# The start of a fused decoder layer: first products in two parts by feature chunks, and x scaled on GpSimd

## The chip, the core and the metric

The kernel runs on one core of a Trainium2 chip: TensorE (PE) multiplies, VectorE (DVE), ScalarE (ACT) and GpSimd (POOL) work elementwise, and SyncE (SP) issues nearly all DMA loads. The metric is the device time of one execution in microseconds, lower is better.

## The reference, cut to what matters

One layer: a half-step SwiGLU feed-forward, token mixing, a second feed-forward, each behind an RMS norm that is scaled and shifted by vectors of a conditioning `c`. The change lies at the very start, in the norm and in the first feed-forward's first columns.

```python
m = jax.nn.silu(c) @ w_ada + b_ada
sh1, sc1, g1, sh2, sc2, g2, sh3, sc3, g3 = jnp.split(m[:, None, :], N_MOD, axis=-1)
h = modulate(rms_norm(x, n1_g), sh1, sc1)        # n * (1 + scale) + shift
x = x + 0.5 * g1 * swiglu(h, w1_gate, w1_up, w1_down)
```

There are 512 prompt rows and 8 x 8 sample rows (T = 576 tokens), 1024 features (8 chunks of 128) and 2816 feed-forward columns (22 of 128). Arithmetic is float32.

## The kernel before

**Layout.** Features lie on the partitions and tokens in the free dimension, in two halves of H = 288 tokens. A float32 product is made of three passes of a rounded type: each operand is split into a high part (a copy on ACT, step names ending in h) and a low part (a subtraction on DVE, names in l), and TensorE adds high x high, high x low and low x high: `prod` (line 620) does so for four chunks, 12 matmuls of 128x288.

**Pairs.** A feed-forward step takes one gate and one up column block: a pair. Most pairs save an eighth of the matmuls by seven products of sums of operand blocks (`Pair`, steps P1 to P7). The first two do not (`Plain`, line 676): they make the eight products as they stand, from blocks that need no sums, since the operands are only coming in. The operand blocks, by feature half and token half: N11 is minus the first half's first tokens, N1 the difference of the first half's token halves (tx), B21 and B22 the second half's first and last tokens. For pair i, h0a multiplies N11 (weights n11, n21: steps nh, nl), h1a N1 with the same weights, h0b and h1b multiply B21 and B22 with a12, a22 (steps wh, wl). Each of these is 24 matmuls. T2, N3, N4 are for the later pairs (p2..., P1, ...).

**The norm.** x is loaded row-wise and turned (xt), copied to the feature layout (xc, xS); the row norms are spread over all partitions by a matmul with a matrix of ones (rw, line 1046) and copied out to `rowr` (rr). `xr0` to `xr3` multiply two chunks each by `rowr`, 128x1152, on DVE (`Operands.x`, line 507). Shift and scale come from four parts of w_ada, 2 MB each (`First`): mm0 to mm3 multiply part p by silu(c), M copies the result out, tr turns it, m adds it up on DVE (lines 300, 304, 363). Part p serves chunks 2p and 2p+1: b (ACT) and s (DVE) then scale and shift these. In an operand block, index j stands for two chunks; N11 and N1 have j = 0, 1 (parts 0, 1), B21 and B22 have 2, 3.

**What sets the order.** The string `BEGIN` lists the steps; `run` calls them in that order and binds each of ACT, DVE, PE and GpSimd to it, so each engine works strictly in the order written, and one step that waits holds all behind it on its engine. SyncE issues loads in the order of construction: parts 0 and 1, pair 0's weights (two 512 KB tiles: first and second feature half), part 2, pair 1's weights, part 3, pair 2's. Raw weights lie in three rotating buffers and one of its own, so a load waits until the split that read its buffer is done. After `BEGIN`, from the third pair on, all follows as one stream; there, matmuls that load further conditioning (w_ada strips, line 319) are woven in.

Of the kernel before, what the change touches and what calls it, by code (L numbers as in the profile page):

```python
# [15 lines left out]
P = 128  # L16
# [6 lines left out]
T = NP + NS  # L23
# [13 lines left out]
HALF = (slice(0, H), slice(H, T))  # L37

BEGIN = """
xt0 xt1 xc0 xt2 xc1 xt3 xc2 xt4 xc3 s5 xt5 xc4 r5 r50 r51 r52 xt6 dg xc5 xt7 xc6 rw xS xc7  # L40
rr xr0 xr3 mm0 xr2 M0 tr0 xr1 mm1 m0 nh0 s0 M1 nl0 b00 tr1 b01 m1 wh0 tx0 b10 s1 b11 wl0
N11h0 N11h1 N11l0 N1h0 N11l1 mm2 tx1 N1l0 N1h1 h0a0 T2a1 M2 N1l1 nh1 T2a0 wh1 nl1 tr2 sn0
h1a0 m2 wl1 b20 b21 s2 B21h2 T2b0 B22h2 h0a1 B21l2 T2h0 N3c0 N4c0 N3h0 T2l0 N4h0 N3l0 mm3
B22l2 sn1 N4l0 M3 tr3 h1a1 m3 b30 s3 b31 B21h3 N3c1 p2ah B21l3 T2b1 h0b1 B22h3 p2al p2bh
T2h1 N3h1 N4c1 B22l3 N4h1 p2S h0b0 T2l1 p2U p2bl p2Sh N3l1 h1b0 p2V N4l1 p2Sl e0s0 e0s1 e0m0
e0m1 h1b1 e1a0 p2Uh e1t0 e1s0 p2Ul e1m0 Gh0 P1 e1a1 e1t1 e1s1 Gl0 P2 e1m1 P1s Gh1 Gl1 P5 P6
P5s P6s
"""
INTO_MIX = """
D00 D01 rs00 Wh2 sp00 sq00 ad00 Wl2 D10 rs01 px0 Wh3 sq01 ad01 Wl3 D11 sp01 rs10 sp10 sq10  # L50
# [29 lines left out]
def layer_kernel(ctx: ExitStack, tc: tile.TileContext, a):  # L80
    nc = tc.nc
    PE, DVE, ACT, POOL = nc.tensor, nc.vector, nc.scalar, nc.gpsimd
# [22 lines left out]
    def nm(s):  # L105
        count[0] += 1
        return f"{s}_{count[0]}"
# [5 lines left out]
    def pool(stack, name, side="left"):  # L113
        return stack.enter_context(tc.tile_pool(name=nm(name), bufs=1, side=side, reuse_waits="tile"))
# [14 lines left out]
    def nine(home, shape, dt=F32R):  # L129
        return now[home].tile(shape, dt, tag="x", name=nm(home), bufs=4 if home == "xa" else 3)  # L130
# [4 lines left out]
    def bank():  # L135
        return pp.tile([P, 512], F32, tag="ps", name=nm("ps"), bufs=8)


    def raw4(shape):
        turn[0] += 1  # L140
        own = now["wraw"] is not None and turn[0] % 4 == 0
        return (now["wraw"] if own else wp).tile(
            [P] + shape, F32, tag="wraw", name=nm("wraw"), bufs=1 if own else 3
        )
# [6 lines left out]
    def load_raw(src, k0, kc, c0, cols):  # L151
        raw = raw4([kc, cols])
        nc.sync.dma_start(
            out=raw, in_=src[k0 * P:(k0 + kc) * P, c0:c0 + cols].rearrange("(k p) c -> p k c", p=P)
        )
        return raw
# [52 lines left out]
    def tick(us):  # L209
        for s in list(side):  # L210
            s[1] -= us
            while s in side and s[1] <= 0:
                try:
                    s[1] += next(s[0])
                except StopIteration:
                    side.remove(s)
# [12 lines left out]
    xreg, hreg, greg = ExitStack(), ExitStack(), ExitStack()  # L229
# [4 lines left out]
    def x2(p):  # L234

        return xall[:, 2 * p:2 * p + 2]
# [29 lines left out]
    for i in range(2):  # L266
        for n in range(NT):
            rows = P if n < 4 else NS
            t = first.tile([rows, 512], F32, name=nm("xt"))
# [61 lines left out]
    class First:  # L331

        def __init__(self, p):
            self.p, self.ws = p, []
            for k in range(KC):
                if k % 4 == 0:
                    e = nine("xa" if p < 2 or (p, k) == (3, 4) else "xs1", [P, 4, 512], F32)
                w = e[:, k % 4]
                nc.sync.dma_start(
                    out=w.rearrange("p (m c) -> p m c", m=2),  # L340
                    in_=a["w_ada"][0, k * P:(k + 1) * P, :].rearrange("p (m c) -> p m c", m=9)[
                        :, 0:2, p * 256:(p + 1) * 256],
                )
                self.ws.append(w)
# [126 lines left out]
    def cost(kc):  # L471
        return kc * 3 * 0.1225
# [20 lines left out]
    def op(name):  # L493
        if name not in ops:
            t = nine("xs1" if name in ops["near"] else "xa", [P, 2, 4, H])
            ops[name] = t[:, 0], t[:, 1]
        return ops[name]

    class Operands:
# [6 lines left out]

        def x(self, p, r, cl):
            n = cl.stop - cl.start
            DVE.tensor_tensor(
                out=self.hb[:, 2 * p:2 * p + 2, cl], in0=x2(p)[:, :, cl],  # L510
                in1=r.unsqueeze(1).broadcast_to([P, 2, n]), op=ALU.mult,
            )
# [56 lines left out]
    def operand_steps(O):  # L569
        st = {}  # L570
        for j in range(2):
            for n in ("T2", "N3", "N4", "N1"):
                st[f"{n}h{j}"] = lambda n=n, j=j: O.hi(n, j)
                st[f"{n}l{j}"] = lambda n=n, j=j: O.lo(n, j)
            for n in ("B21", "B22"):
                st[f"{n}h{j + 2}"] = lambda n=n, j=j: O.hi(n, j)
                st[f"{n}l{j + 2}"] = lambda n=n, j=j: O.lo(n, j)
            st[f"N11h{j}"] = lambda j=j: O.hi("N11", j)
            st[f"N11l{j}"] = lambda j=j: O.lo("N11", j)
            st[f"tx{j}"] = lambda j=j: O.tx(j)  # L580
            for n in ("T2a", "T2b", "N3c", "N4c"):
                st[f"{n}{j}"] = lambda n=n, j=j: O.sums(n, j)
        for p in range(4):
            st[f"s{p}"] = lambda p=p: O.s(p)
        return st
# [11 lines left out]
                else:  # L597
                    st[f"b{p}{c}0"] = lambda p=p, c=c: O.b(2 * p + c, HALF[0])

    def pair_steps(p, greg):  # L600

        st = {}

        def G(i, f):
            if now.get("slf") is not greg:
                greg.close()
                now["sl"], now["slots"], now["slf"] = pool(greg, "slf", "right"), FSLOT, greg
            f(i)

        for i in range(2):  # L610
            for n, f in (("nh", "nh"), ("nl", "nl"), ("wh", "wh"), ("wl", "wl"), ("h0a", "h0a"), ("sn", "snaps"),
                         ("h1a", "h1a"), ("h0b", "h0b"), ("h1b", "h1b"), ("e0s", "e0s"), ("e0m", "e0m"),
                         ("e1a", "e1a"), ("e1s", "e1s"), ("e1t", "e1t"), ("e1m", "e1m")):
                st[f"{n}{i}"] = lambda i=i, f=f: getattr(p[i], f)()
            st[f"Gh{i}"] = lambda i=i: G(i, lambda i: p[i].finish_hi())
            st[f"Gl{i}"] = lambda i=i: G(i, lambda i: p[i].finish_lo())
        for n in ("p2ah", "p2al", "p2bh", "p2bl", "p2S", "p2Sh", "p2Sl", "p2U", "p2V", "p2Uh", "p2Ul"):
            st[n] = lambda n=n: getattr(p[2], n[2:])()
        for n, f in (("P1", "p1"), ("P2", "p2"), ("P5", "p5"), ("P6", "p6"), ("P1s", "p1s"), ("P5s", "p5s"), ("P6s", "p6s")):
            st[n] = lambda f=f: getattr(p[2], f)()  # L620
        return st

    def prod(ps, w, x, fresh):
        (wh, wl), (xh, xl) = w, x
        for j in range(4):
            for z, (s, m) in enumerate(((wh, xh), (wh, xl), (wl, xh))):
                PE.matmul(  # L627
                    ps[:, :H], lhsT=s[:, j * P:(j + 1) * P], rhs=m[:, j, :],
                    start=fresh and j == 0 and z == 0, stop=j == 3 and z == 2, skip_group_check=True,
                )  # L630
        tick(cost(4))

    def snap(ps, t=None):
        if t is None:
# [41 lines left out]
    class Plain(Weights):  # L676


        def __init__(self, cols, n):
            self.cols, self.n, self.g, self.w, self.hl, self.raw = cols, n, None, {}, {}, []  # L680
            for z in range(2):
                t = raw4([2, 4, P])
                for i in range(2):
                    self.block_of(t[:, i], i, z)
                self.raw.append(t.rearrange("p m k c -> p m (k c)"))

        def nh(self):
            self.put_hi(("n11", "n21"), self.raw[0], True)
# [226 lines left out]
    class Down:  # L915
# [5 lines left out]
        def load(self, c):  # L921
            if c not in self.raw:
                self.raw[c] = load_raw(self.wd, self.f0, self.n, c * P, P)
# [72 lines left out]

    w1 = a["w1_gate"][0], a["w1_up"][0]
    a1 = lines(cst, [P, KC, 9], name="a1")
    parts = [First(0), First(1)]
    def cols(w, f):  # L1000
        return (w[0], f * P), (w[1], f * P)

    pairs = {0: Plain(cols(w1, 0), 0)}
    parts.append(First(2))
    pairs[1] = Plain(cols(w1, 1), 1)
    parts.append(First(3))
    pairs[2] = Pair(cols(w1, 2))
    junk = ada_tile()
    for i in range(2):
        for n in range(NT):  # L1010
            m = P if n < 4 else NS
# [18 lines left out]
    s5, r5, t5 = (lines(tp, [P, NT], tag=f"n{i}", name=f"n{i}", bufs=1) for i in range(3))  # L1030
    rowr = tp.tile([P, T], F32, tag="all", name="rowr", bufs=1)
    dg, psR = [], []
# [31 lines left out]
            return getattr(O1(), name)  # L1064

    ops["near"] = ("B21", "B22", "N3")
    steps = {**operand_steps(Late()), **pair_steps(pairs, greg)}
    for c in range(KC):
        steps[f"xt{c}"] = lambda c=c: turn_x(c)
        steps[f"xc{c}"] = lambda c=c: DVE.tensor_copy(out=xs[c][:, 0:NP], in_=psX[c])  # L1070
# [31 lines left out]
    tok_pools, st, xxreg = ExitStack(), ExitStack(), ExitStack()  # L1102
# [609 lines left out]
    for i in range(2):  # L1712
        for n in range(NT):
            m, z = P if n < 4 else NS, NT * i + n
# [71 lines left out]
    xt2 = []  # L1786
# [17 lines left out]
    for pr in ([0], [1], [2], [3], [4], [5], [6, 7]):  # L1804
# [4 lines left out]
        for h in range(2):  # L1809
            for c in pr:  # L1810
                ps = proj(W[c], OA, h)
                t = sa[c][:, HALF[h]]
# [22 lines left out]
    ffn2, st = ExitStack(), ExitStack()  # L1835
    hreg, greg = ExitStack(), ExitStack()
# [19 lines left out]
    pairs = {0: Plain(cols(w2, 0), 0), 1: Plain(cols(w2, 1), 1), 2: Pair(cols(w2, 2))}  # L1856
    steps = {**operand_steps(O), **pair_steps(pairs, greg)}
# [173 lines left out]
```

## Time and profile before

| | us |
|---|---|
| median of 3 runs (1686.89 to 1688.15) | 1687.76 |
| the profiled execution | 1688.23 |
| its span, first to last instruction | 1686.4 |
| TensorE busy | 1650.3 (98%) |
| VectorE busy | 1157.2 (69%) |
| ScalarE busy | 785.5 (47%) |
| GpSimd busy | 290.6 (17%) |
| chain that ended last: TensorE's share | 91% |

The chain that ended last is followed back from the last instruction, each step to what released it. It is almost all TensorE, with DMA 3%. A busy TensorE is not TensorE at its peak, since matmuls are pipelined; start-to-start times tell more than the length of one.

### The profile page before, as it was taken

What the parts mean: (1) busy time and instruction counts of PE and PEld (TensorE: products, weight loads), DVE (VectorE), ACT (ScalarE), POOL (GpSimd) and SP (SyncE); (2) the same over time, 40 slices, a digit from 0 to 9 for tenths busy, and PEclk for the clock granted to TensorE, in tenths of its full rate; (3) what the DMA queues carried; (4) which work ended last, traced back from release to release, by engine and by line L of the source; (5) the groups of instructions that cost most, each with busy time, mean ns of one, the idle gap of its engine ahead of it and who ended that gap; (6) DMA issues with size and microseconds to landing.
All of it is one profiled execution on the core that took longest, in us unless ns stands there. A gap on an engine that the chain in (4) does not pass through costs nothing.

```text
span 1686.4 us, 31365 instructions
## 1 busy us (share of the span) xinstructions
PE 1650.3 (98%) x12548; PEld 1589.0 (94%) x12548; DVE 1157.2 (69%) x1835; ACT 785.5 (47%) x1331; POOL 290.6 (17%) x372
## 2 busy tenths in 40 slices
PE   8999999999999999999999999999999999999997
PEld 4899999999999998899999999998999999999997
DVE  6767847576697776754687654676848868676773
ACT  6533524344564565553444444443236525343453
POOL 0000000000411110113335442444231000000002
PEclk9999999999999999999999999999999999999999
DMA  9443444332547675665457475789540333232331
GB/s 317 130 149 101 139 142 121 113 114 85 166 127 226 202 217 170 210 197 180 127 180 241 156 171 170 205 232 283 182 138 3 96 91 95 87 96 77 100 88 57
DMA packets 300213, 252.09 MB, mean 149 GB/s; under 512 B 13594, under 2 KB 260634, under 8 KB 300067
## 3 DMA queue, kind: packets, MB, share of 16 engines
q1 hardware_dynamic: 284594, 206.76, 40.2%
q0 software_dynamic: 13168, 40.97, 8.8%
q10 hardware_dynamic: 2304, 2.36, 0.4%
q8 instruction: 98, 1.61, 0.4%
q14 instruction: 49, 0.39, 0.1%
HBM read 207.01 MB, written 43.02 MB: 148 GB/s over the span
## 4 chain that ended last, share of the span: by engine, by line
PE 91%; DMA 3%; DVE 2%; issue 1%; ACT 1%; SPq 1%; POOL 0%; DVEq 0%; POOLq 0%; ACTq 0%
PE ps L627 46%; PE ps L461 29%; PE ps L1325 5%; PE ps L1553 2%; PE ps L283 2%; PE ps L1453 1%; PE ps L1336 1%; PE ps L1415 1%; DMA xa<-in_w_ada_dram 1%; PE ps L1459 1%; PE ps L1431 0%; PE ps L1353 0%; PE ps L295 0%; DMA c<-in_gm_ln_g_dram 0%; DMA c<-accd 0%
## 5 line engine op out<-in xcount | busy, mean ns | idle before, releaser
L627 PE MATMUL ps<-xa,whl 128*128 128x288 f32 x3000 | 429.5, 298 | 4.5 <-ACT whl L645 1.4
L627 PEld LDWEIGHTS ps<-xa,whl 128*128 128x128 f32 x3000 | 410.1, 190 | 17.3 <-issue 5.9
L627 PE MATMUL ps<-xs,whl 128*128 128x288 f32 x2040 | 294.1, 297 | 4.0 <-ACT sn L636 4.0
L627 PEld LDWEIGHTS ps<-xs,whl 128*128 128x128 f32 x2040 | 278.8, 189 | 13.9 <-ACT sn L636 6.8
L655 DVE TENSOR_TENSOR whl<-wraw,whl 128x1024 fp32r<-128x1024 f32 x192 | 234.6, 1225 | 57.5 <-ACT whl L645 50.3
L645 ACT CAST whl<-wraw 128x1024 fp32r<-128x1024 f32 x192 | 200.4, 1048 | 104.0 <-DVE wraw L769 60.2
L461 PE MATMUL ps<-c,wd 128*128 128x288 f32 x1824 | 246.1, 295 | 0.0
L461 PEld LDWEIGHTS ps<-c,wd 128*128 128x128 f32 x1824 | 242.9, 188 | 3.4 <-issue 3.4
L461 PE MATMUL ps<-c,whl 128*128 128x288 f32 x1368 | 191.6, 297 | 4.3 <-DVE S L1492 3.2
L461 PEld LDWEIGHTS ps<-c,whl 128*128 128x128 f32 x1368 | 183.3, 188 | 7.0 <-DVE S L1492 3.9
L448 POOL TENSOR_TENSOR x<-x,s 128x64 f32<-128x64 f32 x72 | 35.0, 487 | 817.0 <-DVE s L447 789.5
L442 DVE SCALAR_TENSOR_TENSOR x<-ps,gate,x 128x288 f32<-128x288 f32 (+1 forms) x128 | 61.2, 481 | 119.3 <-PE ps L461 119.3
L165 DVE TENSOR_TENSOR whl<-wraw,whl 128x1024 fp32r<-128x1024 f32 x56 | 80.1, 1433 | 72.5 <-ACT whl L164 70.0
L636 ACT COPY sn<-ps 128x288 f32<-128x288 f32 x195 | 77.6, 398 | 109.4 <-PE ps L627 108.5
L928 ACT CAST wd<-wraw 128x640 fp32r<-128x640 f32 (+2 forms) x58 | 45.3, 781 | 106.7 <-PE ps L461 102.1
L1325 PE MATMUL ps<-whl,xx 128*128 128x256 f32 x768 | 91.6, 279 | 0.0
L1325 PEld LDWEIGHTS ps<-whl,xx 128*128 128x128 f32 x768 | 90.7, 188 | 0.0
L164 ACT CAST whl<-wraw 128x1024 fp32r<-128x1024 f32 x56 | 58.6, 1048 | 28.2 <-PE ps L461 16.0
L627 PE MATMUL ps<-xs,whs 128*128 128x288 f32 x480 | 70.1, 294 | 0.0
L645 ACT CAST whs<-wraw 128x512 fp32r<-128x512 f32 x62 | 38.4, 620 | 66.1 <-PE ps L627 58.9
L627 PEld LDWEIGHTS ps<-xs,whs 128*128 128x128 f32 x480 | 65.7, 188 | 0.0
L933 DVE TENSOR_TENSOR wd<-wraw,wd 128x640 fp32r<-128x640 f32 (+2 forms) x58 | 53.4, 921 | 9.0 <-ACT wd L928 8.6
(285 smaller groups left out, 2226.6 us busy)
## 6 DMA issues: line engine op xcount, KB each, us to landing
ada<-in_w_ada_dram SPq DMA_DIRECT2D x56, 512.0 KB
wraw<-in_w_in_dram SPq DMA_DIRECT2D x96, 256.0 KB
wraw<-in_w_gate_dram SPq DMA_DIRECT2D x88, 256.0 KB
wraw<-in_w_up_dram SPq DMA_DIRECT2D x88, 256.0 KB
wraw<-in_w_in_dram SPq DMA_DIRECT2D x32, 512.0 KB
wraw<-in_w_down_dram SPq DMA_DIRECT2D x32, 384.0 KB
wraw<-in_w_down_dram SPq DMA_DIRECT2D x32, 320.0 KB
accd<-c POOLq DMA_DIRECT2D x32, 288.0 KB, 5.5
```

Source lines behind the costliest of these rows:

```text
L164: ACT.copy(out=hi, in_=raw)
L165: (eng or DVE).tensor_tensor(out=lo, in0=raw, in1=hi.bitcast(F32), op=ALU.subtract)
L442: DVE.scalar_tensor_tensor(out=x[:, o:o + w], in0=ps[:, :w], scalar=g[:, c, 0:1], in1=x[:, o:o + w], op0=ALU.mult, op1=ALU.add)
L448: return lambda: POOL.tensor_tensor(out=x[:, NP:T], in0=x[:, NP:T], in1=u, op=ALU.add)
L461: PE.matmul(ps[:, :H], lhsT=s[:, k, c0:c0 + P], rhs=m[:, HALF[h]], start=k == 0 and z == 0, stop=k == kc - 1 and z == 2,)
L627: PE.matmul(ps[:, :H], lhsT=s[:, j * P:(j + 1) * P], rhs=m[:, j, :], start=fresh and j == 0 and z == 0, stop=j == 3 and z == 2, skip_group ...
L636: ACT.copy(out=t, in_=ps[:, :H])
L645: ACT.copy(out=hl[:, 0], in_=src)
L655: DVE.tensor_tensor(out=hl[:, 1], in0=src, in1=hl[:, 0].bitcast(F32), op=ALU.subtract)
L928: ACT.copy(out=hl[:, 0], in_=self.raw[c])
L933: DVE.tensor_tensor(out=lo, in0=self.raw[c], in1=hi.bitcast(F32), op=ALU.subtract)
L1325: PE.matmul(ps[:, :DV], lhsT=s, rhs=m, start=i == 0, stop=i == 23)
```

## The change

Four things, all before 80 us. (1) Each product of the first two pairs is cut in two by feature chunks: h0a has only the chunks j = 0, h0c those of j = 1, h1a and h1c likewise; h0b, h0d, h1b, h1d for the second half. Each is 12 matmuls; their number and sum stay the same. (2) The pairs' weights are loaded part by part: first halves behind parts 0 and 1, second halves behind parts 2 and 3. (3) `BEGIN` is written anew. (4) `xr1`, `xr2`, `xr3` run on GpSimd, `xr0` stays on DVE; the later norms, which call `x` by token halves, stay on DVE too.

```diff
-            DVE.tensor_tensor(
+            (POOL if p and cl.stop == T and not cl.start else DVE).tensor_tensor(
                 out=self.hb[:, 2 * p:2 * p + 2, cl], in0=x2(p)[:, :, cl],
...
-    def pair_steps(p, greg):
+    def pair_steps(p, greg, parted=False):
...
         for i in range(2):
+            if parted:
+                for n in ("h0a", "h0c", "h0b", "h0d", "h1a", "h1c", "h1b", "h1d"):
+                    st[f"{n}{i}"] = lambda i=i, n=n: p[i].part(n)
...
-                st[f"{n}{i}"] = lambda i=i, f=f: getattr(p[i], f)()
+                st.setdefault(f"{n}{i}", lambda i=i, f=f: getattr(p[i], f)())
...
-    def prod(ps, w, x, fresh):
+    def prod(ps, w, x, fresh, js=range(4)):
...
-        for j in range(4):
+        for j in js:
...
-        tick(cost(4))
+        tick(cost(len(js)))
...
+        def part(self, name):
+
+            t = "AD"[int(name[1])]
+            z, js = {"a": (0, (0, 1)), "c": (0, (2, 3)), "b": (1, (0, 1)), "d": (1, (2, 3))}[name[2]]
+            if name[2] == "a":
+                setattr(self, t, [bank() for _ in range(2)])
+            x = (("N11", "B21"), ("N1", "B22"))[int(name[1])][z]
+            for ps, w in zip(getattr(self, t), (("n11", "n21"), ("a12", "a22"))[z]):
+                prod(ps, self.w[w], op(x), z == 0, js)
...
-    parts = [First(0), First(1)]
...
-    pairs = {0: Plain(cols(w1, 0), 0)}
-    parts.append(First(2))
-    pairs[1] = Plain(cols(w1, 1), 1)
-    parts.append(First(3))
+    pairs, parts = {i: Plain(cols(w1, i), i, ()) for i in range(2)}, []
+    for p in range(4):
+        parts.append(First(p))
+        pairs[p % 2].load(p // 2)
     pairs[2] = Pair(cols(w1, 2))
```

In the lists below, each row is an instruction with its line, output<-inputs and size; line numbers of the changed kernel differ a little. TensorE before, from the ones matmul to the first products (xa_150 and xa_155 are part 0, the next two part 1, xs_28 and xs_29 part 2; xa_370 with whl_343 is h0a of pair 0):

```order
L1046 MATMUL ps_295<-h_284,ones 128x64
L283 MATMUL ps_312<-xa_150,cs 32x512 x4
L283 MATMUL ps_312<-xa_155,cs 32x512 x4
L295 MATMUL ps_324<-ident,ada_322 128x128 x4
L283 MATMUL ps_330<-xa_160,cs 32x512 x4
L283 MATMUL ps_330<-xa_165,cs 32x512 x4
L295 MATMUL ps_351<-ident,ada_347 128x128 x4
L283 MATMUL ps_377<-xs_28_176,cs 32x512 x4
L283 MATMUL ps_377<-xs_29_181,cs 32x512 x4
L627 MATMUL ps_390<-xa_370,whl_343 128x288 x12
```

And now (xa_350 is N11, xa_376 is N1, whl_321 the weights n11 and n21):

```order
L282 MATMUL ps_294<-xa_155,cs 32x512 x4
L1061 MATMUL ps_303<-h_276,ones 128x128
L1061 MATMUL ps_303<-h_278,ones 128x128
L1061 MATMUL ps_303<-h_280,ones 128x128
L1061 MATMUL ps_303<-h_282,ones 128x128
L1061 MATMUL ps_304<-h_284,ones 128x64
L294 MATMUL ps_314<-ident,ada_310 128x128 x4
L282 MATMUL ps_336<-xa_163,cs 32x512 x4
L282 MATMUL ps_336<-xa_168,cs 32x512 x4
L294 MATMUL ps_354<-ident,ada_352 128x128 x4
L630 MATMUL ps_362<-xa_350,whl_321 128x288 x6
L630 MATMUL ps_363<-xa_350,whl_321 128x288 x6
```

mm0 has moved ahead of the ones matmuls, and the first products ahead of mm2. VectorE before, at the multiplications by the norms (hb is the normed x, m, mT and a belong to step m0, whl to nl0):

```order
L509 TENSOR_TENSOR hb_309<-x_90,rowr 128x1152 x4
L300 TENSOR_REDUCE m_339<-ps_324 128x36
L304 TENSOR_TENSOR mT<-m_339,vec 128x2x18
L363 SCALAR_TENSOR_TENSOR a_149<-mT,vec 128x18
L525 TENSOR_TENSOR hb_309<-hb_309,a_149 128x2x64
L525 TENSOR_TENSOR hb_309<-hb_309,mT 128x2x64
L651 SCALAR_TENSOR_TENSOR whl_343<-wraw_170,whl_343 128x1024
```

And now; the other three multiplications stand on GpSimd as `L508 TENSOR_TENSOR hb_331<-x_90,rowr 128x1152 x3`, with nothing ahead of them but the memsets of the start:

```order
L299 TENSOR_REDUCE m_323<-ps_314 128x36
L303 TENSOR_TENSOR mT<-m_323,vec 128x2x18
L362 SCALAR_TENSOR_TENSOR a_149<-mT,vec 128x18
L508 TENSOR_TENSOR hb_331<-x_90,rowr 128x1152
L654 SCALAR_TENSOR_TENSOR whl_321<-wraw_160,whl_321 128x1024
L524 TENSOR_TENSOR hb_331<-hb_331,a_149 128x2x64
L524 TENSOR_TENSOR hb_331<-hb_331,mT 128x2x64
L546 SCALAR_TENSOR_TENSOR xa_350<-hb_331,xa_350 128x576
```

m0 has moved ahead of x0, and one multiplication is left on VectorE. ScalarE before, where wh1 stands (`whl_423`, right behind nh1 `whl_420`; ada_417 is M2, sn are copies of finished products):

```order
L289 COPY ada_417<-ps_377 128x512
L643 ACTIVATE whl_420<-wraw_186 128x1024
L645 CAST whl_423<-wraw_189 128x1024
L636 COPY sn_431<-ps_390 128x288
L636 COPY sn_433<-ps_391 128x288
```

And now (ada_540 is M3, the two activations are b30 and b31, whl_576 is wh1, xs_82 is B21h3):

```order
L288 COPY ada_540<-ps_531 128x512
L541 CAST xs_89_544<-hb_331 128x576
L541 CAST xa_556<-hb_331 128x576
L515 ACTIVATE hb_331<-hb_331,mT,a_149 128x512 x2
L648 CAST whl_576<-wraw_199 128x1024
L541 CAST xs_82_493<-hb_331 128x576
```

wh1 has moved behind M3 and behind b30 and b31.

More of the change, by code (lines that the diff above doesn't have):

```diff
@@ L39 @@
 BEGIN = """
[L40 to L47, printed above, removed]
+xt0 xt1 xc0 xt2 xc1 xt3 xc2 xt4 xc3 s5 xt5 xc4 r5 r50 r51 r52 xt6 dg xc5 xt7 xc6 mm0 rw M0 xS xc7 tr0
+rr nh0 m0 xr0 xr1 xr2 xr3 mm1 nl0 b00 b01 s0 N11h0 M1 tr1 N11l0 tx0 h0a0 N1h0 m1 N1l0 b10 b11 s1 h1a0
+N11h1 N11l1 tx1 N1h1 h0c0 N1l1 nh1 sn0 nl1 h1c0 mm2 M2 T2a0 T2a1 h0a1 wh0 tr2 m2 h0c1 wl0 b20 b21 s2
+B21h2 B21l2 sn1 B22h2 T2b0 h0b0 B22l2 T2h0 N3c0 h1b0 mm3 M3 N4c0 T2l0 N3h0 tr3 N3l0 m3 N4h0 b30 b31
+h1a1 s3 wh1 N4l0 B21h3 wl1 B21l3 h1c1 B22h3 N3c1 B22l3 h0b1 p2ah T2b1 h0d0 p2al T2h1 h1d0 p2bh N3h1 T2l1
+h1b1 N4c1 h0d1 e0s0 p2S N3l1 N4h1 e0s1 p2U e0m0 p2bl p2Sh h1d1 N4l1 e0m1 p2V e1a0 p2Sl p2Uh
+e1t0 e1s0 p2Ul P1 e1m0 Gh0 e1a1 e1t1 e1s1 Gl0 P2 e1m1 P1s Gh1 Gl1 P5 P6 P5s P6s
 """
@@ L676, in layer_kernel, with __init__, load @@
     class Plain(Weights):
-        def __init__(self, cols, n):
+        def __init__(self, cols, n, halves=range(2)):
             self.cols, self.n, self.g, self.w, self.hl, self.raw = cols, n, None, {}, {}, []
[L681 to L685, printed above, removed]
+            for z in halves:
+                self.load(z)
+        def load(self, z):
+            t = raw4([2, 4, P])
+            for i in range(2):
+                self.block_of(t[:, i], i, z)
+            self.raw.append(t.rearrange("p m k c -> p m (k c)"))
+        def part(self, name):
[6 more added lines that the diff above has]
+                prod(ps, self.w[w], op(x), z == 0, js)
         def nh(self):
@@ L1066, in layer_kernel @@
     ops["near"] = ("B21", "B22", "N3")
-    steps = {**operand_steps(Late()), **pair_steps(pairs, greg)}
+    steps = {**operand_steps(Late()), **pair_steps(pairs, greg, True)}
     for c in range(KC):
```

## The prediction, made before the changed kernel had run

> **What bounds the kernel now.** I read the busy times by stretch first: they cut the start at the places where TensorE's work changes. Columns: stretch, its length, busy time of each engine, then the granted clock, the DMA share and GB/s.
>
> ```profile
> core 0: us, PE busy (x) PEld busy (x) DVE busy (x) ACT busy (x) POOL busy (x), PEclk, DMA share, GB/s
> 18.40:34.50 16.10, 14.19 (x67) 5.06 (x66) 15.57 (x27) 8.96 (x14) 0.00 (x0) 1.00 1.06 345
> 34.50:46.60 12.10, 12.10 (x93) 10.46 (x92) 9.09 (x16) 7.56 (x12) 0.00 (x0) 1.00 1.08 345
> 46.60:49.20 2.60, 0.65 (x9) 0.59 (x6) 2.10 (x3) 1.77 (x5) 0.00 (x0) 1.00 0.92 302
> 49.20:52.60 3.40, 3.40 (x16) 3.40 (x15) 2.23 (x7) 2.48 (x4) 0.00 (x0) 0.50 0.59 155
> 52.60:66.60 14.00, 14.00 (x106) 14.00 (x106) 13.33 (x21) 8.03 (x12) 0.00 (x0) 1.00 0.14 40
> 66.60:115.80 49.20, 49.20 (x363) 44.33 (x362) 33.32 (x52) 24.14 (x41) 0.00 (x0) 1.00 0.47 137
> ```
>
> From 18.4 to 49.2 the DMA engines are full (share 0.92 to 1.08); VectorE is full until 34.5 (15.57 of 16.10); GpSimd does nothing. From 52.6 on TensorE has no gap. So the change can move the time only by when TensorE gets through the first two pairs: what it is late there, it is late at the end. The next view is TensorE in order of time (start, duration, what, and in brackets the idle time before).
>
> ```profile
> 18.08 0.37 PE L1024 MATMUL ps<-ident,xt 64*128 64x64 f32 x1
> 18.37 2.69 PE L1046 MATMUL ps<-h,ones 128*128 128x128 f32 x10
> 20.99 2.33 PE L283 MATMUL ps<-xa,cs 128*32 128x512 f32 x16
> 24.12 0.66 PE L295 MATMUL ps<-ident,ada 128*128 128x128 f32 x4 [0.79 <-ACT ada L289]
> 24.70 1.92 PE L283 MATMUL ps<-xa,cs 128*32 128x512 f32 x16
> ...
> 32.88 1.71 PE L283 MATMUL ps<-xs,cs 128*32 128x512 f32 x4 [0.27 <-DMA xs<-in_w_ada_dram]
> 34.52 3.46 PE L627 MATMUL ps<-xa,whl 128*128 128x288 f32 x24
> 37.81 0.60 PE L295 MATMUL ps<-ident,ada 128*128 128x128 f32 x4
> 38.17 6.63 PE L627 MATMUL ps<-xa,whl 128*128 128x288 f32 x48
> ...
> 48.61 0.66 PE L295 MATMUL ps<-ident,ada 128*128 128x128 f32 x4 [1.96 <-ACT ada L289]
> 49.02 4.96 PE L627 MATMUL ps<-xa,whl 128*128 128x288 f32 x24
> 53.82 12.96 PE L627 MATMUL ps<-xs,whl 128*128 128x288 f32 x96
> 66.62 1.76 PE L627 MATMUL ps<-xa,whl 128*128 128x288 f32 x12
> ```
>
> The first product stands at 34.52, behind the third part's DMA; the two pairs have 24+48+24+96 = 192 product matmuls; the third pair begins at **66.62**. 96 of them take 66.62 - 53.82 = 12.80 (0.133 each), 48 take 6.56 (0.137): I use 0.1345. Check: 34.52 + 192 x 0.1345 (25.8) + mm3 1.9 + two turns 1.1 + the wait 1.96 + what the half clock adds to 24 matmuls (4.80 to the next start, against 3.3: 1.5) = 66.8, against 66.62. This sum, made again for the new order, is the forecast.
>
> **The change: the first product without GpSimd's price.** Prices of the small steps:
>
> ```profile
> 20.48 0.59 ACT L1051 COPY rowr<-ps 128x512 f32<-128x512 f32 x1 [3.48 <-PE ps L1046]
> 21.10 0.21 ACT L1052 COPY rowr<-ps 128x64 f32<-128x64 f32 x1
> 39.23 1.52 ACT L516 ACTIVATE hb<-hb,mT,a 128x512 f32<-128x512 f32 x2 [0.82 <-DVE a L363]
> 33.98 0.67 ACT L542 CAST xa<-tx 128x576 fp32r<-128x576 f32 x1 [1.08 <-DVE tx L559]
> 34.62 0.59 ACT L289 COPY ada<-ps 128x512 f32<-128x512 f32 x1
> 28.73 1.03 ACT L645 CAST whl<-wraw 128x1024 fp32r<-128x1024 f32 x1
> 21.34 5.16 DVE L509 TENSOR_TENSOR hb<-x,rowr 128x1152 f32<-128x1152 f32 x4 [0.28 <-ACT rowr L1052]
> 38.45 0.31 DVE L300 TENSOR_REDUCE m<-ps 128x36 f32<-128x144 f32 x1 [0.69 <-PE ps L295]
> 38.79 0.20 DVE L304 TENSOR_TENSOR mT<-m,vec 128x36 f32<-128x36 f32 x1
> 39.02 0.18 DVE L363 SCALAR_TENSOR_TENSOR a<-mT,vec 128x18 f32<-128x18 f32 x1
> 39.53 1.23 DVE L655 TENSOR_TENSOR whl<-wraw,whl 128x1024 fp32r<-128x1024 f32 x1 [0.33 <-issue]
> 40.67 0.28 DVE L525 TENSOR_TENSOR hb<-hb,a 128x128 f32<-128x128 f32 x1
> 42.07 0.75 DVE L551 TENSOR_TENSOR xs<-hb,xs 128x576 fp32r<-128x576 f32 x1
> ```
>
> mm0 now stands ahead of rw on TensorE. Together they took 18.37 to 23.3 and still do, but rowr is copied out at 23.4 to 24.2, 2.9 us later than at 20.48. tr0 ends at 24.0, m0 (0.31 + 0.20 + 0.18 with links, 0.75) at 24.9, x0 (5.16 / 4 = 1.29) at 26.2, b00 and b01 (1.52) at 27.7, N11h0 (0.67) at 28.4. Behind it on ScalarE M1 (0.59) ends at 29.0 and tr1 on TensorE at 29.7; N11l0 (0.75) is done at 29.2. First product: **29.7**, 4.8 earlier than now, because it needs neither the second half of the chunks nor m2.
>
> **GpSimd's three multiplications.** They replace 3 x 1.29 on VectorE. The trace has no 128x1152 row on GpSimd; the nearest are additions of 128x576, with VectorE beside them:
>
> ```profile
> 769.54 0.75 DVE L1302 TENSOR_TENSOR c<-c,rope 128x576 f32<-128x576 f32 x1
> 770.20 3.56 DVE L165 TENSOR_TENSOR whl<-wraw,whl 128x1024 fp32r<-128x1024 f32 x2
> 773.93 0.69 DVE L1355 TENSOR_TENSOR c<-ps,hc 128x512 f32<-128x512 f32 x1 [0.17 <-PE ps L1353]
> ```
>
> ```profile
> 770.36 2.31 POOL L1303 TENSOR_TENSOR c<-c,c 128x576 f32<-128x576 f32 x1 [1.88 <-DVE c L1302]
> 772.74 1.17 POOL L1383 COPY h<-c 128x128 f32<-128x128 f32 x1
> ```
>
> Two instructions of 1.23 take 3.56 beside GpSimd: 1.1 to 1.2 us more than two alone. GpSimd starts at 770.36, within the first, takes 2.31 and ends at 772.67; the first of the two is over by 771.4. I read it as turn-taking: VectorE's first, then GpSimd's whole addition (about 1.3), then VectorE's second, which had to stand still. The 0.69 row, with an operand in PSUM, is as long as ever. The Trainium skill's "GPSIMD Engine Reference", section "Specifications", says that GpSimd shares its SBUF interfaces with VectorE, with contention for VectorE instructions that have two SBUF inputs; it gives no price for the wait. These rows agree. Without that rule the sum below ends at +0.7 us, with it at +8.2.
>
> A 128x1152 multiplication is then, as an estimate from these rows, 2 x 1.3 to 1.35, 2.7 us (bounds: 0 for VectorE if nothing is shared, 2 x 2.31 = 4.6 if the whole row counts; I take 2.7, since the rest of the 2.31 is GpSimd's own wait). All three are ready when rowr is there, at 24.2. VectorE then has mT, a, x0, nl0, s0 (two) and N11l0 to do before the first product, all with two SBUF operands, and they alternate: GpSimd's x1 to 26.9, mT, x2 to 29.8, a, x3 to 32.6, x0 to 33.9. Queued behind mT is all of VectorE, and ScalarE and TensorE wait for that. Then b00, b01 to 35.4, N11h0 36.1, M1 36.6, tr1 and with it the first product at **37.2**: 2.7 later than now, not 4.8 earlier.
>
> **From the first product to the third pair.** h0a0 runs to 38.8. h1a0 waits for tx0, N1h0, N1l0 (0.75 + 0.67 + 0.75, to 39.0): 0.3 idle. h0c0 waits for b10, b11, N11h1, N11l1, to 41.3: 0.6. h1c0 waits for tx1, N1h1, N1l1: 0.6. Now mm2, h0a1, tr2, h0c1 run to 50.8, but h0b0 needs B21l2, and from the end of tr2 (49.2) that is m2 0.75, b20 and b21 1.52, B21h2 0.67, B21l2 0.75 and links 0.4: 53.3, **2.5 idle**; only h0c1 (1.6) covers it. h0b0, h1b0, mm3 run to 58.4; tr3 waits 0.8 for M3. h1a1 and h1c1 run to 63.0; h0b1 needs wl1, and on ScalarE wh1 (1.03) stands behind b30 and b31, on VectorE wl1 (1.23) behind it: m3, b30, b31, wh1, wl1 end at 65.1, **2.1 idle**. The six parts left, with no wait, are 9.7.
>
> Sum: 37.2 + 25.8 + mm2 and mm3 3.8 + two turns 1.1 + waits (0.3 + 0.6 + 0.6 + 2.5 + 0.8 + 2.1 = 6.9) = **74.8** against 66.6: +8.2 us. The third pair then follows with no new wait: laid out by the same rows, its p2al, p2bl and p2Sl are ready 6, 3 and 1.5 us ahead.
>
> **Moves that I cost at nothing.** SyncE's loads: 512 KB of weights now stand ahead of part 1, at 345 GB/s 1.5 us; mm1 ends near 26, and tr1 is not due before 29.7. Part 2 lands as before (33.5 by the 32.88 row), mm2 comes at 45. Part 3 lands 1.5 us earlier, to no use: mm3 comes at 56. The early landing is not what TensorE waits for any more; without the cover of the late start, part 1's delay would cost 1.5. Pair 3's second weight tile is queued behind the two w_ada strips, whose buffers wait for tr2 and tr3 (59.8), and for wl1 (65.1); it lands near 68 and is wanted near 77.
>
> **Rivals.** (1) *GpSimd costs VectorE nothing*: first product 29.7, the same 37.6 behind it, 67.4, **+0.7**. For it: nothing but that a multiplication by a broadcast row may pass otherwise than these additions. Against: the 3.56. (2) *Faster*: the early start is kept, if there is no turn-taking and the waits in front of h0b0 and h0b1 (4.6) and the small ones shrink to 1.5, as VectorE has 3.9 us less to do: 62, **-4.6**. It decides at a chain from tr2 to B21l2 below h0c1's 1.6; the rows make it 4.1, in the trace of before too. (3) *Part of the turns*: one or two of three fall behind VectorE's work: **+3 to +6**. (4) *Half clock*: now 1.96 idle is followed by 3.4 us at 0.50, at a cost of 1.5; the idle times of 2.5 and 2.1 may each bring one: **up to +11**. The Trainium skill's "TensorE: Matmul & The Clock Gate", Part 1, lets the clock fall after an idle window of about 3.4 us: by it these two cost nothing, and only the 10 us ahead of the first product would, hidden in the small waits. The row of 1.96 speaks against so strict a reading.
>
> **The numbers.** The profiled execution took 1688.23 (span 1686.40), 0.5 above the median of 1687.76. Forecast +8.2: 1696.4 by that execution, 1696.0 as a median. Chances: forecast 0.48, (4) 0.16, (3) 0.12, (1) 0.14, (2) 0.10. The range goes from (1), 1688.0, to (4), 1699.5; below it lies (2), above it some of (4). A measurement tells 0.2%, 3.4 us, from no change: slower 0.74, same 0.16, faster 0.10.
>
> **What would show it.** Right: VectorE's mT, a and x0 rows stretched to 2 us and more beside three GpSimd rows between 24 and 33 us; first product near 37; waits of over 2 us ahead of h0b0 and h0b1; third pair near 75. Wrong: mT at 0.2 us and a first product at 30; or a TensorE without those two waits.

## The result, and the profile after

The changed kernel takes 1694.74 us (median of 4 runs, 1694.71 to 1695.94) against 1687.35 for the kernel before (4 runs beside it): a ratio of 1.0048, 95% interval 1.0036 to 1.006, or 7.4 us more. Run again later beside other experiments it had the same ratio, 1.0048 (1.0035 to 1.006). The profiled execution took 1695.94, with a span of 1694.2 where the kernel before had 1686.4.

TensorE of the changed kernel in order of time (start, duration, what, idle time before and what ended it):

```profile
18.99 3.64 PE L282 MATMUL ps<-xa,cs 128*32 128x512 f32 x16
22.56 1.56 PE L1061 MATMUL ps<-h,ones 128*128 128x128 f32 x10
...
24.63 1.92 PE L282 MATMUL ps<-xa,cs 128*32 128x512 f32 x16
33.89 1.11 PE L294 MATMUL ps<-ident,ada 128*128 128x128 f32 x4 [7.33 <-ACT ada L288]
34.65 0.59 PE L630 MATMUL ps<-xa,whl 128*128 128x288 f32 x1
35.92 8.34 PE L630 MATMUL ps<-xa,whl 128*128 128x288 f32 x47 [0.68 <-DVE xa L546]
44.19 1.92 PE L282 MATMUL ps<-xs,cs 128*32 128x512 f32 x16
...
51.51 0.40 PE L630 MATMUL ps<-xs,whl 128*128 128x288 f32 x1 [1.56 <-ACT xs L541]
52.30 4.83 PE L630 MATMUL ps<-xs,whl 128*128 128x288 f32 x23 [0.40 <-DVE xs L550]
...
59.78 0.66 PE L294 MATMUL ps<-ident,ada 128*128 128x128 f32 x4 [0.79 <-ACT ada L288]
...
64.35 0.53 PE L630 MATMUL ps<-xs,whl 128*128 128x288 f32 x2 [0.33 <-ACT whl L648]
65.61 9.59 PE L630 MATMUL ps<-xs,whl 128*128 128x288 f32 x70 [0.73 <-DVE whl L658]
75.04 1.76 PE L630 MATMUL ps<-xa,whl 128*128 128x288 f32 x12
```

The first product comes at 34.65, almost where it came before (34.52), and the third pair at 75.04 instead of 66.62. That is 8.4 us later, and the span grew by 7.8: the loss lies in the first 75 us. The stretches between these rows (length, busy time of each engine, granted clock, DMA share, GB/s):

```profile
core 0: us, PE busy (x) PEld busy (x) DVE busy (x) ACT busy (x) POOL busy (x), PEclk, DMA share, GB/s
18.40:34.65 16.25, 8.92 (x53) 3.77 (x52) 11.97 (x10) 4.92 (x8) 9.01 (x3) 0.84 1.10 375
34.65:44.19 9.54, 8.86 (x51) 8.27 (x49) 7.38 (x16) 5.10 (x8) 0.00 (x0) 0.73 0.75 244
44.19:52.30 8.11, 6.15 (x46) 4.27 (x45) 4.20 (x10) 4.57 (x8) 0.00 (x0) 1.00 0.30 88
52.30:57.07 4.77, 4.77 (x24) 4.61 (x24) 3.29 (x5) 1.00 (x2) 0.00 (x0) 0.64 0.62 187
57.07:75.04 17.97, 15.99 (x118) 13.79 (x117) 13.29 (x23) 11.78 (x17) 0.00 (x0) 1.00 0.21 59
75.04:124.24 49.20, 49.20 (x359) 43.98 (x358) 37.20 (x59) 24.91 (x43) 0.00 (x0) 1.00 0.49 148
```

In the 49.20 us behind 75.04 TensorE has no gap, as before behind 66.62. From the first product to the third pair there lie 192 matmuls of 0.1345 us (25.8), mm2 and mm3 (3.8) and two turns (1.1), 30.7 in all; the stretch took 40.39, so 9.7 is waits and half clock. Before, mm2 stood ahead of the first product, and the same stretch was 32.10 for 28.8 of work: 3.3. The loss is thus 0.1 (first product) + 1.9 (mm2, now inside) + 6.4. VectorE and GpSimd ahead of the first product:

```profile
24.74 0.31 DVE L299 TENSOR_REDUCE m<-ps 128x36 f32<-128x144 f32 x1 [4.21 <-PE ps L294]
25.08 2.19 DVE L303 TENSOR_TENSOR mT<-m,vec 128x36 f32<-128x36 f32 x1
27.31 2.52 DVE L362 SCALAR_TENSOR_TENSOR a<-mT,vec 128x18 f32<-128x18 f32 x1
29.75 1.34 DVE L508 TENSOR_TENSOR hb<-x,rowr 128x1152 f32<-128x1152 f32 x1
31.01 3.65 DVE L654 SCALAR_TENSOR_TENSOR whl<-wraw,whl 128x1024 fp32r<-128x1024 f32 x1
...
35.11 0.75 DVE L546 SCALAR_TENSOR_TENSOR xa<-hb,xa 128x576 fp32r<-128x576 f32 x1
```

```profile
24.57 9.01 POOL L508 TENSOR_TENSOR hb<-x,rowr 128x1152 f32<-128x1152 f32 x3 [22.59 <-DMA xa<-in_w_ada_dram]
```

mT, a and nl0 took 0.20, 0.18 and 1.22 before; now 2.19, 2.52 and 3.65, 6.8 more, while GpSimd works on its three multiplications (9.01 in all). x0 between them keeps its 1.34.

### The profile page after: what moved, and what is told of

Read it like the earlier page. It is cut to its first block, busy times and chain, and to the rows that moved or that the text cites. A ratio compares the mean times of both kernels' runs of the same rounds, so it can differ in the third digit from the quotient of the medians.

```text
span 1694.2 us, 31383 instructions
## 1 busy us (share of the span) xinstructions
PE 1649.6 (97%) x12548; PEld 1588.8 (94%) x12548; DVE 1159.3 (68%) x1832; ACT 784.2 (46%) x1331; POOL 299.7 (18%) x375
## 4 chain that ended last, share of the span: by engine, by line
PE 85%; issue 6%; DMA 4%; DVE 3%; ACT 1%; POOL 1%; SPq 1%; POOLq 0%; DVEq 0%; ACTq 0%
PE ps L630 39%; PE ps L460 30%; PE ps L1340 5%; PE ps L1568 2%; PE ps L282 1%; PE ps L1468 1%; PE ps L1351 1%; PE ps L1430 1%; DMA c<-x1d 1%; DMA xa<-in_w_ada_dram 1%; PE ps L1474 1%; DMA accd<-c 1%; PE ps L1446 0%; PE ps L1368 0%; DMA c<-in_gm_ln_g_dram 0%
```

## The experiments

Theory T: GpSimd's turns, and where the multiplications, mm2 and wh1 stand, make the loss. Rival O: GpSimd costs VectorE nothing; the order alone loses. Rival C: half clock, which the changed kernel has for 10.24 us from 29.49 and for 3.41 from 53.38 (before: 3.41 from 49.18). Rival P: cutting the products is what loses. All ratios are to the kernel before, on the same chip. The third pair's start, and the time at half clock ahead of it, are those of one profiled execution of each kernel.

| run | third pair at, us | half clock ahead of it, us | ratio | 95% interval |
|---|---|---|---|---|
| before | 66.62 | 3.41 | 1 | |
| changed | 75.04 | 13.65 | 1.0048 | 1.0036 to 1.006 |
| e8, changed again | 72.78 | 10.24 | 1.0048 | 1.0035 to 1.006 |
| e1, x on VectorE | 70.34 | 6.83 | 1.0034 | 1.0022 to 1.0046 |
| e2, before with GpSimd | 66.06 | 0 | 1.0012 | 1.0004 to 1.0021 |
| e3, rows first | 72.88 | 10.24 | 1.005 | 1.0038 to 1.0062 |
| e4, TensorE kept busy | 74.13 | 3.41 | 1.0065 | 1.0051 to 1.0079 |
| e5, x ahead of its use | 68.12 | 3.41 | 1.0012 | 1.0003 to 1.0022 |
| e6, and wh1 early | 65.79 | 3.41 | 0.9996 | 0.9987 to 1.0005 |
| e7, order by rows | 60.91 | 0 | 0.9969 | 0.9956 to 0.9981 |
| e9, e7 with GpSimd | 65.64 | 6.83 | 1.0007 | 0.9997 to 1.0018 |

In the extracts of `BEGIN` below, lines are shortened to the steps that move.

**e1: the multiplications back on VectorE.**

```diff
-            (POOL if p and cl.stop == T and not cl.start else DVE).tensor_tensor(
+            DVE.tensor_tensor(
```

> The changed kernel with the three multiplications x1 to x3 back on VectorE, at the same places. Theory T (GpSimd's turns stretch VectorE's instructions): mT and a back at 0.2 us, VectorE has 3 x 1.29 = 3.9 us more of its own but loses 2.0 + 2.3 + 2.4 = 6.7 us of stretching; the first product near 32.5 instead of 34.65, the third pair near 70.5 to 71.5 instead of 75.0, so 3.5 to 4.5 us faster than the changed kernel, still 3 to 4 us slower than the kernel before. Rival O (GpSimd costs VectorE nothing, the order alone makes the loss): VectorE is 3.9 us longer ahead of the first product, up to 3.9 us slower than the changed kernel. Rival C (half clock): no change beyond what the half-clock stretches do; the loss stays while there are 13.6 us of half clock.

VectorE of this run:

```profile
23.94 0.20 DVE L303 TENSOR_TENSOR mT<-m,vec 128x36 f32<-128x36 f32 x1
24.17 0.18 DVE L362 SCALAR_TENSOR_TENSOR a<-mT,vec 128x18 f32<-128x18 f32 x1
24.57 5.16 DVE L508 TENSOR_TENSOR hb<-x,rowr 128x1152 f32<-128x1152 f32 x4 [0.23 <-DMA wraw<-in_w_gate_dram]
29.66 1.22 DVE L654 SCALAR_TENSOR_TENSOR whl<-wraw,whl 128x1024 fp32r<-128x1024 f32 x1
```

The stretching is gone and nl0 ends at 30.88, not 34.66, though VectorE does three multiplications more. One matmul of the first product runs at 29.14, the others from 32.13, 3.8 earlier than in the changed kernel. The third pair is 4.7 earlier than in the first profile of the changed kernel and 2.4 earlier than in the second; like this run, the second has no half clock behind the wait ahead of h0b0. O, which had this run slower, falls. But the ratio is still 1.0034: without GpSimd the new order loses too.

**e2: only GpSimd, in the old order.** The same edit as the change's, in the kernel before.

> The kernel before with nothing but x1 to x3 on GpSimd. Theory T: mT, a and an instruction behind them are stretched by some 2 us each, the third pair starts near 69.5 instead of 66.6, 2 to 4 us slower than before. Rival O: VectorE is relieved of 3.9 us, no change or up to 2 us faster.

```profile
26.09 1.41 DVE L304 TENSOR_TENSOR mT<-m,vec 128x36 f32<-128x36 f32 x1
27.53 2.54 DVE L363 SCALAR_TENSOR_TENSOR a<-mT,vec 128x18 f32<-128x18 f32 x1
```

In these rows of VectorE the two instructions are stretched by 1.2 and 2.4, less than the 3.9 that VectorE is spared, and the first product comes at 34.76, where it came before at 34.52. The expected 69.5 was too late: in the old order part 2's load and mm2 stand ahead of the first product and cover most of it. What is left is 0.9 us, by which the turn behind the first 24 products starts later (38.74 against 37.81). The ratio says 0.4 to 2.1 in a thousand slower, but the third pair is 0.6 earlier, because this profile has no half clock behind the 1.96 us of idle time, worth 1.5 before. T's sign holds by the times; its size was over-estimated.

**e3: rows ahead of mm0.**

```diff
-xc6 mm0 rw M0 xS xc7 tr0
-rr nh0 m0
+xc6 rw mm0 xS xc7 rr M0
+tr0 nh0 m0
```

> The changed kernel with the ones matmuls (rw) and the copies of rowr ahead of mm0 and M0, as before the change. rowr is there 2.9 us earlier, so GpSimd's first multiplication falls into VectorE's idle time in front of m0 and takes no turn from it. Theory T: one turn less, the third pair near 72.3, 2 to 3 us faster than the changed kernel. Rival O: the multiplications were not what the first product waited for, less than 1 us. Rival C: no change.

```profile
25.18 0.31 DVE L299 TENSOR_REDUCE m<-ps 128x36 f32<-128x144 f32 x1 [4.61 <-PE ps L294]
25.52 1.08 DVE L303 TENSOR_TENSOR mT<-m,vec 128x36 f32<-128x36 f32 x1
26.64 2.51 DVE L362 SCALAR_TENSOR_TENSOR a<-mT,vec 128x18 f32<-128x18 f32 x1
29.08 1.34 DVE L508 TENSOR_TENSOR hb<-x,rowr 128x1152 f32<-128x1152 f32 x1
30.35 1.21 DVE L654 SCALAR_TENSOR_TENSOR whl<-wraw,whl 128x1024 fp32r<-128x1024 f32 x1
```

The turns went as T said: GpSimd's first multiplication (from 21.31) falls into VectorE's idle time, mT loses only 0.9, and nl0 nothing. The time is a miss all the same: ratio 1.005, no better. mm0 now waits behind rw, and m0 starts at 25.18, against 24.74 and 23.14 in the two profiles of the changed kernel. Against the first of them the third pair is 2.2 earlier, about as expected. Against the second it is no earlier: VectorE's last split ahead of mm2 ends at 40.41, only 0.5 before its 40.87, and a half-clock stretch ahead of the third pair, worth 1.5, fell into this profile and not into that one. Against this second profile, then, the later m0 takes back most of what the earlier rowr wins, and the times show no gain.

**e4: TensorE kept busy.**

```diff
-rr nh0 m0 xr0 xr1 xr2 xr3 mm1 nl0
+rr nh0 m0 xr0 xr1 xr2 xr3 mm1 dm0 nl0
...
-tr2 m2 h0c1 wl0
+tr2 m2 h0c1 dm1 wl0
...
+        for _ in range(20):
+            PE.matmul(parts[1].p2[:, 0:P], lhsT=ones, rhs=ident, start=True, stop=True)
...
+        for _ in range(4):
+            PE.matmul(pairs[1].A[0][:, H:H + P], lhsT=ones, rhs=ident, start=True, stop=True, skip_group_check=True)
```

The second batch is written with `start=True` into the bank in which pair 1's first sums are being added up. The output suggests that this starts the bank's sum anew, so that a part of pair 1's product is left out.

> The changed kernel with matmuls of ones by the identity, whose results nobody reads, in two of TensorE's idle times: 20 behind mm1 (about 6.8 us of the 7.3) and 4 behind h0c1 (about 1.4 us). The granted clock should then stay at 1.0 in the first 75 us. Rival C (half clock makes the loss): the 48 products behind the first take 6.5 instead of 9.5 us and the 24 behind the second idle time 3.3 instead of 5, so 3 to 5 us faster than the changed kernel. Theory T: VectorE's chain behind the stretched instructions holds mm2 at about 43.9 whatever the clock, and the second stretch is given back in the wait ahead of tr3 or h0b1: 0 to 1 us faster.

The windows of this run, cut at the same places:

```profile
18.40:36.66 18.26, 13.54 (x93) 8.40 (x92) 13.91 (x13) 4.92 (x8) 7.82 (x3) 0.97 1.10 375
36.66:44.79 8.13, 7.82 (x50) 7.42 (x49) 5.79 (x12) 5.09 (x8) 0.00 (x0) 0.86 0.59 186
...
52.90:56.16 3.26, 3.26 (x24) 3.09 (x24) 3.26 (x5) 1.00 (x2) 0.00 (x0) 1.00 0.80 259
```

Half clock ahead of the third pair fell from 13.65 us to 3.41, yet mm2 starts at 44.79, 0.6 later than in the changed kernel. The last matmuls ahead of it need a split that VectorE ended at 43.08 here and at 42.48 there; mm2 follows it by 1.71 us in both. So the first stretch at half clock cost nothing in that profile. VectorE was late for a reason of its own: the third turn fell on x0 this time, where the changed kernel had it on nl0.

```profile
29.26 3.84 DVE L508 TENSOR_TENSOR hb<-x,rowr 128x1152 f32<-128x1152 f32 x1
33.02 1.21 DVE L654 SCALAR_TENSOR_TENSOR whl<-wraw,whl 128x1024 fp32r<-128x1024 f32 x1
```

The 23 matmuls behind the second idle time take 3.26 instead of 4.77, and this 1.5 reaches the third pair in full: I had expected it to be given back in later waits. So C explains 1.5 us of one profile, and e8, whose ratio is the same, ran these 23 matmuls in 3.26 by itself. The whole time is a miss: the third pair is 0.9 earlier, yet the profiled execution needs 1623.5 us from there to the end, 4.3 more than the changed kernel's. This is idle time of TensorE (30.5 us behind the third pair, against 26.0). Two waits make up 2.5 of it, 1.03 us ahead of the product at 212.48 and 1.43 ahead of that at 313.83, for ScalarE's copies of finished products (sn); no other run has such waits there. ScalarE had before waited for a load of down-projection weights, for 1.35 and 1.50 us. Why these loads come late in this run stays open.

**e5 and e6: the multiplications ahead of their use, then wh1 earlier.** All on VectorE, with cut parts and loads as changed.

```diff
-mm0 rw M0 xS xc7 tr0 rr nh0 m0 xr0 xr1 xr2 xr3 mm1 nl0
+rw mm0 xS xc7 rr xr0 M0 tr0 nh0 xr1 m0 mm1 nl0
...
-nl1 h1c0
+nl1 xr2 xr3 h1c0
```

> The changed kernel in its cut parts and its order of loads, with the four multiplications on VectorE, rw ahead of mm0, x0 ahead of m0 (in VectorE's idle time), x1 behind it, and x2 and x3 only behind nl1, shortly ahead of their first use. Theory T (the loss is where GpSimd's and VectorE's multiplications stand, ahead of the first product; the cut parts and the loads cost nothing): first product near 29.5, third pair near 67, so 8 us faster than the changed kernel and within 2 us of the kernel before. Rival P (cutting the product into parts by feature chunks is itself what loses, since each part waits for its own splits): no better than the run with the multiplications on VectorE at their old place, third pair near 70 or later.

e6 has in addition:

```diff
-mm3 M3 N4c0 T2l0 N3h0 tr3 N3l0 m3 N4h0 b30 b31 h1a1 s3 wh1 N4l0 B21h3 wl1
+mm3 M3 wh1 N4c0 T2l0 N3h0 tr3 m3 N4h0 b30 b31 h1a1 s3 wl1 N3l0 N4l0 B21h3
```

> The run before it with one move more: wh1 right behind M3 on ScalarE, ahead of b30 and b31, and wl1 ahead of N3l0 and N4l0. Theory T: the waits ahead of h0b1 (0.3 + 0.7 us in the changed kernel) and what they hide go, third pair near 65, 2 us earlier than the run before it and 1 to 2 us earlier than in the kernel before. If wh1's place is not what h0b1 waits for: no change, third pair near 67.

In e5 the first product comes at 29.25, as expected, and the third pair at 68.12, 1.1 later than expected, with 3.41 us of half clock behind the wait ahead of h0b0. The cut parts as such lose nothing like 8 us: P falls. But a first product 5.3 us earlier than in the kernel before is not enough by itself: mm2 (1.9) stands behind it now, and the waits ahead of h0b0 and h0b1 are still there. e6 takes the second away:

```profile
52.51 0.66 PE L294 MATMUL ps<-ident,ada 128*128 128x128 f32 x4 [0.78 <-ACT ada L288]
52.92 3.44 PE L630 MATMUL ps<-xa,whl 128*128 128x288 f32 x24
56.20 9.76 PE L630 MATMUL ps<-xs,whl 128*128 128x288 f32 x72
```

h0b1 follows h1c1 without a wait, where TensorE in e5 still had 0.28 and 0.73; the third pair is 2.3 earlier, about as expected; 0.4 of this is there at the first product already (28.85 against 29.25).

**e7: an order laid out by the rows.** BEGIN is written anew with the rows' durations so that each split stands shortly ahead of its use and mm2, M2 and tr2 come in the midst of pair 0. Its core:

```diff
-N11h1 N11l1 tx1 N1h1 h0c0 N1l1 nh1 sn0 nl1 h1c0 mm2 M2 T2a0 T2a1 h0a1 wh0 tr2 m2 h0c1 wl0 b20 b21 s2
...
+h1a0 mm2 T2a0 N1h1 N1l1 N11h1 xr2 h1c0 N11l1 M2 tr2 h0c0 nl1 wh0 h0a1 T2a1 m2 xr3 b20 s2 wl0 b21 sn0
```

> The same cut parts and loads, everything on VectorE, in an order laid out with the durations of the rows so that no engine waits for another behind the first product: all four multiplications and all splits shortly ahead of their use, mm2 and tr2 ahead of the second half of pair 0, the splits of the third pair earlier. Theory T: TensorE without idle time from the first product (29.5) on, third pair at 60.5 to 62.5, 4 to 6 us faster than the kernel before (ratio 0.9965 to 0.9975). Rival C (half clock): if TensorE's idle time ahead of the first product brings half clock whatever follows, up to 3.4 us of that is lost. Rival P: third pair not ahead of 66.6.

```profile
core 0: us, PE busy (x) PEld busy (x) DVE busy (x) ACT busy (x) POOL busy (x), PEclk, DMA share, GB/s
18.40:30.12 11.72, 9.20 (x51) 4.12 (x51) 8.31 (x14) 5.48 (x9) 0.00 (x0) 1.00 1.10 376
30.12:60.91 30.79, 30.79 (x236) 27.44 (x235) 29.72 (x50) 22.10 (x35) 0.00 (x0) 1.00 0.69 219
```

From the first product at 30.12 to the third pair TensorE is busy for 30.79 of 30.79 us, about the 30.7 of work counted above, at full clock. The ratio of 0.9969 is 4 to 5 us less than the kernel before takes, with the change's cut products and loads.

**e9: e7 with x1 to x3 on GpSimd**, the change's edit and nothing else.

> The order laid out by rows, which had the third pair at 60.9, with nothing changed but x1 to x3 on GpSimd again. Theory T: rowr is there at 21.4, so one of the three multiplications (2.6 to 3.0 us each) falls into VectorE's idle time; of the other two, one holds up mT or a and one an instruction behind it, by 2 to 2.6 us each; tr1 and the first product come 3 to 4 us later, TensorE behind them has no slack left to hide it, third pair at 64 to 65.5, 3 to 4.5 us slower than the same order on VectorE. Rival O (GpSimd costs VectorE nothing, and takes 3.9 us off it): the third pair at 60.9 or earlier, no slower.

```profile
25.20 0.31 DVE L299 TENSOR_REDUCE m<-ps 128x36 f32<-128x144 f32 x1 [2.37 <-PE ps L294]
25.54 2.43 DVE L303 TENSOR_TENSOR mT<-m,vec 128x36 f32<-128x36 f32 x1
28.00 2.51 DVE L362 SCALAR_TENSOR_TENSOR a<-mT,vec 128x18 f32<-128x18 f32 x1
30.55 0.29 DVE L524 TENSOR_TENSOR hb<-hb,a 128x128 f32<-128x128 f32 x1
```

```profile
21.52 8.96 POOL L508 TENSOR_TENSOR hb<-x,rowr 128x1152 f32<-128x1152 f32 x3 [19.56 <-DMA xa<-in_w_ada_dram]
```

The first multiplication is hidden, the second and third hold up mT and a by 2.2 and 2.3, all behind them comes later, and with nothing to hide it the third pair goes from 60.91 to 65.64. This is the clearest price of the GpSimd edit: 4.7 us there, and a ratio that goes from 0.9969 to 1.0007, with intervals that don't overlap. About 0.8 of the 4.7 is half clock that began in the longer idle time: the first 24 products take 4.31 us, against 3.53 in e7.

**e8: the changed kernel again.** No edit.

> The changed kernel once more, on the chip of the three runs beside it, so that they are compared with it directly: a ratio to the kernel before of 1.004 to 1.006, a third pair at 74 to 76, and half clock for 7 to 14 us in the first 60 us.

Its third pair, at 72.78, is 1.2 earlier than I had allowed. m0 starts 1.6 earlier there (mm0 took 2.55 instead of 3.64), and the second half-clock stretch, worth 1.5, is missing; 10.38 instead of 9.54 for the first 48 products takes 0.8 back.

## Why the prediction was right

The mechanism held: GpSimd's multiplications stretched small instructions of VectorE, this took away the early first product, and the two long waits behind it came where they were forecast. That the third pair agrees to 0.2 us (74.8 forecast, 75.04 in the profile) is in part luck, since two errors largely cancel: mm2 came at 44.19 and not at 45, and a half-clock stretch that the sum left out cost 1.5 behind it. The second profile of the same kernel, without that stretch, had 72.78.

- **GpSimd's turns: right in kind, a little long in size.** I took 2.7 us for each of three turns; VectorE's instructions were stretched by 2.0, 2.3 and 2.4. e1 and e9 show that this is the multiplications' doing. Rival (1), that GpSimd costs nothing, is refuted.
- **The order of the turns: wrong for the changed kernel.** The prediction let x3 go ahead of x0. In both its traces x0 had its turn first, and x3 ran beside nl0 (3.65 and 3.64 us), with ScalarE already at b00. The first product came not at 37.2 but at 34.65 with one matmul, and at 35.92 with the rest. In e4 the third turn fell on x0 as forecast, and the first product came at 36.66. What decides between the two is not shown.
- **rw behind mm0: its two sides were not weighed.** I booked rowr's 2.9 us delay as a pure cost, though the sum also had m0 come earlier for it. e3 puts what the move cost at 2.2 us of the third pair's start against one profile of the changed kernel and at nothing against the other, and its times show no difference.
- **The waits behind the first product: right.** The sum counts from start to start. So counted, the wait ahead of h0b0 cost 2.4 (2.5 forecast), that ahead of tr3 0.8 (0.8), and that ahead of h0b1 1.9 (2.1). The idle times in the rows, 1.56 + 0.40 and 0.33 + 0.73, are shorter, since they begin only where the length given for the last matmul ends. That wh1's place makes the last wait was shown by e6; that the chain from mm2 by tr2 and m2 makes the first fits e7, where mm2 starts earlier and the wait is gone.
- **Half clock: kept out of the sum, and it came.** Rival (4) had it; the changed kernel had 13.65 us of it. The first 48 products took 9.54 instead of the 8.0 of my sum, yet e4 shows that at full clock VectorE would have held mm2 as late. In e8 mm2 follows the split by 2.56 us instead of 1.71, so there half clock ahead of mm2 cost 0.8. The second stretch cost 1.5 in the first profile, and the kernel before paid as much in its own. So the loss against before is not half clock, and the +11 of rival (4) was too high.
- **Two slips in the sums** change nothing: the turns are counted at 1.1 by their lengths, where their starts and the next ones lie 0.8 apart in all, and rival (1)'s 29.7 + 37.6 is 67.3, not 67.4.
- **Moves costed at nothing: right.** In the first 75 us of the changed kernel no matmul from mm1 on waited for a DMA, and pair 3's weights came in time, since TensorE is busy for 49.20 of 49.20 us behind the third pair.
- **Rival (2), faster, named the right point**: the chain from tr2 to B21l2. This order doesn't cover it; e7 does, with mm2 some 10 us earlier (33.65), and with the multiplications off GpSimd it is faster than the kernel before.

Taken apart by the times: e1 leaves 3.4 of the 4.8 thousandths with the new order, and gives 1.4 to GpSimd, with intervals that overlap. In the denser order of e7 and e9 GpSimd's price is 3.8 thousandths. The same edit costs 1.2 in the old order. So the price depends on the order: on how much else there is to hide the turns.

## What to carry to other kernels

Moving an elementwise instruction to an idle engine pays only if the busy engine can run beside it: a tiny instruction with two operands in SBUF that is queued ahead of everything waits for a whole large one on GpSimd. Before moving work off an engine, see whether that work can stand later on it, shortly ahead of its use; here e5, which does this (with rw ahead of mm0 again), was faster than the changed kernel (1.0012 against 1.0048). An earlier first product is worth little while later waits remain: in e5 it came 5.3 us earlier than in the kernel before, and the third pair 1.5 later. Follow each wait to its chain and start that chain earlier.

## What the runs showed of the hardware

VectorE's reduction at L299, with its only input in PSUM, took 0.31 us in the midst of GpSimd's work, while the sum of 128x36 right behind it, with two operands in SBUF, took 2.43 (e9). The Trainium skill's "SBUF — State Buffer", section "Who interferes with whom", says that an instruction of VectorE with two SBUF inputs contends with a GpSimd instruction that reads SBUF, that a reduction never does on trn2, and that the one who comes first holds the port for the whole instruction. The rows agree with the first and the third; a reduction that reads PSUM alone can't tell whether the second holds for SBUF inputs. They add that the two engines took turns one instruction at a time, and that the third turn fell on nl0 in both profiles of the changed kernel (3.65 and 3.64 us) and on x0 in e4 (3.84).

GpSimd waits too: its three multiplications took 7.82 us where x0 didn't fall among them (e3 and e4), and 8.96 to 9.01 where it did (the changed kernel, e2, e8 and e9), about 1.2 more for the 1.34 of x0.

Half clock came in stretches of 3.41 us or two or three times that (6.83 in e1, 10.24 in the changed kernel), and not always: the wait of 1.96 us in the old order was followed by a stretch in the kernel before and by none in e2, and that of 1.56 in the changed kernel in one profile of two. A stretch of 3.41 us that fell on products cost 1.5. Runs of the same kernel differ by such stretches: of 17 runs of the kernel before on one chip the shortest, 1683.3 us, had a mean granted clock of 0.997 and the longest, 1689.08, one of 0.993, and 0.004 of 1686 us is 6.7, close to the 5.8 between them. The Trainium skill's "TensorE: Matmul & The Clock Gate", Part 1, puts the window at about 3.4 us; the length of the stretches agrees, but here stretches also followed idle times of 2 us and less.
